# Keeping the split weight panels of the first token block in DRAM and loading them in the other three

## The chip, the cores and the metric

The kernel runs on one core of a Trainium2 chip. TensorE (PE) multiplies, VectorE (DVE), ScalarE (ACT) and GpSimd (POOL) do the elementwise work, and SyncE (SP) issues the DMAs, which all run on the core's 16 DMA engines. The metric is the time of one execution on the device in microseconds, the median of several; lower is better. Numbers are float32 throughout.

## The reference

One decoder layer works on 2048 tokens of width 1024. Cut to what matters here:

```
xn = RMSNorm(h);  z = xn @ W_in
o  = concat(GLA(z_gla), RWKV7(z_rwkv)) @ W_out ;  h += o
h += relu(RMSNorm(h) @ W1)^2 @ W2
h += sigmoid(RMSNorm(h) @ W_g) * (p @ W_p)
out = RMSNorm(h)
```

W1 is 1024 x 4096 and W2 4096 x 1024. GLA and RWKV7 are recurrent mixers that go through the tokens in order.

## The kernel before, in words

The tokens are cut into four blocks (0 to 3) of 512. All weights are cut into panels of 128 x 1024 numbers (512 KB): per block 26 of W_in (stage z), 8 of W_out (o), 64 of W1 and W2 (f) and 10 of W_g and W_p (p), that is 108 panels, and each is used once in each of the four blocks.

A matmul is done with float32r operands, a rounded form of float32 that goes faster. To keep the precision, each operand is split into a rounded part `hi` and the rest `lo`, and each product is three matmuls (L267 to L269): hi x hi, hi x lo, lo x hi. A panel is 8 such products of 128 x 128 against 512 tokens, so 24 matmuls. `load_w` (L237) fetches a panel to `wr` (3 buffers) and splits it in two halves: a cast on ACT to `wh` (L244) and a subtraction to `wl` (L247), on DVE, or in stage z in turn on DVE and POOL. `wh` and `wl` have 5 half-panel buffers each. This happens anew in every block, 432 times in all.

The order of the work: first stage z of block 0; then z of blocks 1 to 3, with the mixers of block 0 woven in between (`tick`, twice per panel); then the o, f and p stages of block 0, with the mixers of block 1 woven in; and so on; those of block 3 have no mixer beside them. Names in the trace begin with stage and block: z2, f0; r12 is the RWKV mixer of block 1, part 2 of 0 to 3, and g12 the GLA mixer of the same part. A part of the RWKV mixer computes an inverse row by row on DVE (L868, L871), writes it to DRAM in eight DMAs (`place`, L887 and L888), reads it back in another layout in ten (tiles `TT` and `rT`), and PE goes on with it (`join`, L913).

The program is written in this order, and a scheduler then fixes the order of the instructions of each engine before the run: each engine executes its list in order and waits at the first instruction whose operands, buffers or (for DMAs, in eight lanes in turn) an earlier DMA of its lane are not ready. All DMAs are on SP's list: weights, tokens, the mixers' operands, results. So an SP instruction that waits holds all transfers behind it.

Of the kernel before, what the change touches and what calls it, by code (L numbers as in the profile page):

```python
# [61 lines left out]
def tile_hybrid_block(ctx: ExitStack, tc: tile.TileContext, a: dict, out: bass.AP):  # L62
# [35 lines left out]

# [1 line left out]
    vec = ct([P, NV], "vec")  # L100
# [71 lines left out]

    # low-rank factors, split into exact float32r parts
    w2s = cx(TB, F32R)[:96]
# [22 lines left out]

# [1 line left out]
    gst = ct([P, 4, P], "gst")  # L199
# [15 lines left out]

# [1 line left out]
    def rsqrt(v, n, tag):  # L217
# [13 lines left out]

    loaded = []

    def take_w():
        return loaded.pop(0)

    def load_w(src):  # L237
        raw = st([P, 1024], "wr", 3)
        ld(raw, src)
        parts = []  # L240
        for x in range(2):
            r = raw[:, 512 * x : 512 * x + 512]
            hi, lo = st([P, 512], "wh", 5, F32R), st([P, 512], "wl", 5, F32R)
            A.copy(hi, r)  # L244
            eng = G if wcount[0] % 2 and stage[0][0] == "z" else V
            wcount[0] += 1
            eng.tensor_tensor(out=lo, in0=r, in1=hi, op=ALU.subtract)  # L247
            parts.append((hi, lo))
        return parts

    def xt():
# [66 lines left out]

# [1 line left out]
    lastc = {}  # L320
# [3 lines left out]
    def z_units(b):  # L324
# [264 lines left out]

        wz = a["w_z"]  # L590
        units += [(low_a, wz[NZ]), (low_b, wz[NZ + 1])]
# [5 lines left out]

# [1 line left out]
    def gla_units(b, j):  # L599
# [161 lines left out]

# [1 line left out]
    NJ = S // P  # L763
    dlt = [tc.dram_tile([32, 32, 32], F32, name=f"dlt{x}") for x in range(NJ)]
    dtt = [tc.dram_tile([32, 32, 32], F32, name=f"dtt{x}") for x in range(NJ)]
    dtp = [tc.dram_tile([16, 32, 32], F32, name=f"dtp{x}") for x in range(NJ)]
    # T^T per head; chunk parity q sits on rows 64 * (1 - q)
    TT = ct([P, 8, 64], "TT")
# [260 lines left out]

# [1 line left out]
    H = {}  # L1031

    def out_units(b):
# [26 lines left out]
        for n in range(KT):  # L1060
            u.append((f_(n), a["w_o"][n]))
        return named(f"o{b}", u)

    def ffn_units(b):
# [30 lines left out]
        def down(g, n):  # L1095
            def f():
                acc = panel(take_w(), s_[g])
                h = H[b]["h"][n]
                V.tensor_tensor(out=h, in0=h, in1=acc, op=ALU.add)
                if g == FF // P // FG - 1:  # L1100
                    H[b]["n"].add(h)
                    H[b]["xs"].append(split_x(h, vc("ln_ple", n)))
            return f

        for g in range(FF // P // FG):
            for i in range(FG):
                u.append((up(g, i), a["w_1"][g * FG + i]))
            for n in range(KT):
                u.append((down(g, n), a["w_2"][g, n]))
        return named(f"f{b}", u)  # L1110

    def ple_units(b):
# [41 lines left out]

        wg, wp = a["w_g"], a["w_p"]
        u.append((first, wg[0], wg[1], wp[0]))
# [156 lines left out]
```

## Time and profile before

| what | value |
|---|---|
| median of 3 timed runs | 2979.53 us (2975.93 to 2981.45) |
| profiled execution, first to last instruction (span) | 2978.2 us |
| TensorE busy | 2869.2 us, 96% |
| VectorE busy | 2295.4 us, 77% |
| ScalarE busy | 1265.4 us, 42% |
| DMA moved | 385.49 MB, 129 GB/s on the mean |

The profile gives the profiled execution's time as its span; nothing is recorded around it, and the timed median is 1.3 us longer. The stages follow each other like this: z0 until about 200 us, z1 to z3 with the mixers of block 0 until about 853, then the o, f and p stages of block 0 until 1395, of block 1 until 1944, of block 2 until 2494 and of block 3 until 2963. In the page, PEclk is the clock that TensorE was granted; 1.00 is 2.4 GHz, and a stretch at the lower level of 1.2 GHz draws the mean down. The DMA share is how busy the 16 DMA engines were.

### The profile page before, as it was taken

How to read it: one execution, taken by the hardware profiler on the slowest of the kernel's cores; microseconds unless marked ns; L12 is line 12 of the kernel's file. 1: busy time of each engine (PE TensorE's matmuls, PEld its weight loads, DVE VectorE, ACT ScalarE, POOL GpSimd, SP SyncE). 2: the span in 40 equal slices, each digit the busy share in tenths (PEclk: the TensorE clock that was granted, in tenths of full speed). 3: DMA queues.
4: the chain of work that ended last, by engine and by line, in shares of the span. 5: the costliest groups of instructions: out<-in, count | busy, mean ns of one | idle time of the engine just before them, and what ended most of it. 6: DMA issues, size and time to landing. Idle time of an engine off the chain costs nothing.

```text
span 2978.2 us, 47104 instructions
## 1 busy us (share of the span) xinstructions
PE 2869.2 (96%) x16856; PEld 2266.4 (76%) x16856; DVE 2295.4 (77%) x5495; ACT 1265.4 (42%) x2382; POOL 214.7 (7%) x347
## 2 busy tenths in 40 slices
PE   8998998899899999999999999999999999999998
PEld 6676776676777778787778778777878787888886
DVE  7899898888988768688968768787867787544455
ACT  6455555556543333344433334443333344322233
POOL 2332221222200000000000000000000000000000
PEclk9999999999999999999999999999999999999999
DMA  4464645544463333444533343454333334322222
GB/s 156 164 189 145 190 133 153 179 141 155 139 200 112 112 118 103 121 121 138 154 119 104 116 117 109 124 179 118 104 116 115 108 109 156 106 92 95 96 92 78
DMA packets 313835, 385.49 MB, mean 129 GB/s; under 512 B 132016, under 2 KB 213984, under 8 KB 313600
## 3 DMA queue, kind: packets, MB, share of 16 engines
q1 hardware_dynamic: 313600, 382.48, 41.2%
q8 instruction: 133, 2.18, 0.3%
q14 instruction: 102, 0.84, 0.1%
HBM read 316.32 MB, written 66.06 MB: 128 GB/s over the span
## 4 chain that ended last, share of the span: by engine, by line
PE 75%; DVE 10%; DMA 2%; issue 2%; ACT 1%; SPq 0%; POOL 0%; DVEq 0%; ACTq 0%; POOLq 0%
PE f0.mm L267 4%; PE f1.mm L267 4%; PE f3.mm L268 4%; PE f3.mm L269 4%; PE f3.mm L267 4%; PE f1.mm L269 4%; PE f0.mm L268 4%; PE f0.mm L269 4%; PE f1.mm L268 4%; PE f2.mm L267 4%; PE f2.mm L269 4%; PE f2.mm L268 4%; PE p1.mm L267 1%; PE p0.mm L267 1%; DVE z3.g L574 1%
## 5 line engine op out<-in xcount | busy, mean ns | idle before, releaser
L244 ACT CAST f3.wh<-f3.wr 128x512 fp32r<-128x512 f32 x128 | 79.5, 621 | 198.7 <-PE f3.mm L268 190.4
L244 ACT CAST f0.wh<-f0.wr 128x512 fp32r<-128x512 f32 x128 | 79.0, 618 | 153.6 <-PE f0.mm L268 121.0
L244 ACT CAST f1.wh<-f1.wr 128x512 fp32r<-128x512 f32 x128 | 79.0, 618 | 147.0 <-PE f1.mm L268 117.2
L244 ACT CAST f2.wh<-f2.wr 128x512 fp32r<-128x512 f32 x128 | 79.0, 618 | 146.1 <-PE f2.mm L268 115.6
L247 DVE TENSOR_TENSOR f3.wl<-f3.wr,f3.wh 128x512 fp32r<-128x512 f32 x128 | 88.0, 688 | 52.9 <-ACT f3.wh L244 52.9
L247 DVE TENSOR_TENSOR f0.wl<-f0.wr,f0.wh 128x512 fp32r<-128x512 f32 x128 | 87.8, 686 | 28.0 <-ACT f0.wh L244 27.9
L247 DVE TENSOR_TENSOR f1.wl<-f1.wr,f1.wh 128x512 fp32r<-128x512 f32 x128 | 87.7, 685 | 27.0 <-ACT f1.wh L244 26.9
L247 DVE TENSOR_TENSOR f2.wl<-f2.wr,f2.wh 128x512 fp32r<-128x512 f32 x128 | 87.7, 685 | 26.5 <-ACT f2.wh L244 26.4
L267 PE MATMUL f2.mm<-f2.x,f2.wh 128*128 128x512 f32 x256 | 103.6, 405 | 0.0
L267 PE MATMUL f1.mm<-f1.x,f1.wh 128*128 128x512 f32 x256 | 103.6, 405 | 0.0
L267 PE MATMUL f0.mm<-f0.x,f0.wh 128*128 128x512 f32 x256 | 103.5, 404 | 0.0
L268 PE MATMUL f1.mm<-f1.x,f1.wh 128*128 128x512 f32 x256 | 101.2, 395 | 0.0
L269 PE MATMUL f1.mm<-f1.x,f1.wl 128*128 128x512 f32 x256 | 101.1, 395 | 0.0
L269 PE MATMUL f0.mm<-f0.x,f0.wl 128*128 128x512 f32 x256 | 101.1, 395 | 0.0
L268 PE MATMUL f0.mm<-f0.x,f0.wh 128*128 128x512 f32 x256 | 101.0, 395 | 0.0
L268 PE MATMUL f2.mm<-f2.x,f2.wh 128*128 128x512 f32 x256 | 100.8, 394 | 0.0
L269 PE MATMUL f2.mm<-f2.x,f2.wl 128*128 128x512 f32 x256 | 100.8, 394 | 0.0
L269 PE MATMUL f3.mm<-f3.x,f3.wl 128*128 128x512 f32 x256 | 100.8, 394 | 0.0
L267 PE MATMUL f3.mm<-f3.x,f3.wh 128*128 128x512 f32 x256 | 100.7, 393 | 0.0
L268 PE MATMUL f3.mm<-f3.x,f3.wh 128*128 128x512 f32 x256 | 100.7, 393 | 0.0
L267 PE MATMUL f0.mm<-o0.x,f0.wh 128*128 128x512 f32 x248 | 100.6, 406 | 0.0
L267 PE MATMUL f1.mm<-o1.x,f1.wh 128*128 128x512 f32 x248 | 100.2, 404 | 0.0
(2804 smaller groups left out, 9164.8 us busy)
## 6 DMA issues: line engine op xcount, KB each, us to landing
f0.wr<-w SPq DMA_DIRECT2D x63, 512.0 KB, 3.3
f1.wr<-w SPq DMA_DIRECT2D x63, 512.0 KB, 3.4
f2.wr<-w SPq DMA_DIRECT2D x63, 512.0 KB, 3.3
f3.wr<-w SPq DMA_DIRECT2D x63, 512.0 KB, 3.3
z0.wr<-w_z SPq DMA_DIRECT2D x27, 512.0 KB, 3.8
z1.wr<-w_z SPq DMA_DIRECT2D x26, 512.0 KB, 3.6
z2.wr<-w_z SPq DMA_DIRECT2D x26, 512.0 KB, 3.9
z3.wr<-w_z SPq DMA_DIRECT2D x25, 512.0 KB, 3.6
```

The source lines that it names most:

```text
L244: A.copy(hi, r)
L247: eng.tensor_tensor(out=lo, in0=r, in1=hi, op=ALU.subtract)
L267: T.matmul(acc, wh, xs[0], start=start, stop=False)
L268: T.matmul(acc, wh, xs[1], start=False, stop=False)
L269: T.matmul(acc, wl, xs[0], start=False, stop=stop)
L574: V.scalar_tensor_tensor(o, x[:, j : j + TB], convh[:, 4 * i + j : 4 * i + j + 1], o, ALU.mult, ALU.add)
```

## The change

In block 0 each panel is loaded and split as before; the two split halves of a panel, now tiles of 128 x 1024 that hold `hi` beside `lo`, are then written to DRAM scratch, 512 KB each. The stores stand in SP's list behind the load of the next panel. In blocks 1 to 3 `load_w` loads these two tiles in place of the raw panel, and nothing is split. The tags `wr`, `wh` and `wl` become one tag `w` with 8 tiles of 4 KB per partition, the same 32 KB per partition as before; block 0 uses three of them per panel, the other blocks two.

```diff
+    wcache = {}
+    pending = []
...
+    def w_tile(dtype):
+        return st([P, 1024], "w", 8, dtype)
+
+    def store_w():
+        while pending:
+            dst, t = pending.pop(0)
+            nc.sync.dma_start(dst, t.bitcast(F32))
+
     def load_w(src):
-        raw = st([P, 1024], "wr", 3)
+        key, src = src
+        parts = []
+        if key in wcache:
+            store_w()
+            for x in range(2):
+                t = w_tile(F32R)
+                ld(t.bitcast(F32), wcache[key][x])
+                parts.append((t[:, :512], t[:, 512:]))
+            return parts
+        raw = w_tile(F32)
         ld(raw, src)
-        parts = []
+        store_w()
+        wcache[key] = []
         for x in range(2):
             r = raw[:, 512 * x : 512 * x + 512]
-            hi, lo = st([P, 512], "wh", 5, F32R), st([P, 512], "wl", 5, F32R)
+            t = w_tile(F32R)
+            hi, lo = t[:, :512], t[:, 512:]
             A.copy(hi, r)
             eng = G if wcount[0] % 2 and stage[0][0] == "z" else V
             wcount[0] += 1
             eng.tensor_tensor(out=lo, in0=r, in1=hi, op=ALU.subtract)
             parts.append((hi, lo))
+            d = tc.dram_tile([P, 1024], F32, name=f"wc_{key[0]}_{'_'.join(map(str, key[1:]))}_{x}")
+            wcache[key].append(d)
+            pending.append((d, t))
         return parts
```

The callers pass a key with each panel (`wsrc`); nothing else changes. The scheduler orders all engines anew. Line numbers after L230 move by 27 (L247 becomes L268, L913 becomes L940).

Three places show it. DVE's list in stage z2, around the convolutions of z2 (L574, later L601; g02 is the GLA mixer beside them), before:

```order
L574 SCALAR_TENSOR_TENSOR z2.g2_1324_5970<-z2.x_1322_5965,convh_96,z2.g2_1324_5970 128x512 [waits DMAHW5_49,Activation_49]
L663 TENSOR_TENSOR g02.gqk_1406_6336<-g02.gk_1277_5779,g02.ge_1405_6332 128x256 [waits PE_49]
L574 SCALAR_TENSOR_TENSOR z2.g2_1324_5970<-z2.x_1322_5965,convh_96,z2.g2_1324_5970 128x512 [waits DVE_49]
L658 TENSOR_TENSOR g02.ge_1407_6342<-g02.gb_1278_5780 128x64x2
L574 SCALAR_TENSOR_TENSOR z2.g2_1324_5970<-z2.x_1322_5965,convh_96,z2.g2_1324_5970 128x512 [waits DVE_49]
L247 TENSOR_TENSOR z2.wl_1372_6192<-z2.wr_1370_6189,z2.wh_1371_6191 128x512 [waits PE_49,Activation_49]
L659 TENSOR_TENSOR g02.ge_1407_6342<-g02.gb_1278_5780 128x64x2
L577 SCALAR_TENSOR_TENSOR z2.g2_1325_5975<-z2.g2_1325_5975,z2.g2_1324_5970 128x512 [waits Activation_49]
L295 TENSOR_TENSOR z3.nacc_1290_5812<-z3.nacc_1290_5812,z3.g2_1334_6028 128x512 [waits Activation_49]
L574 SCALAR_TENSOR_TENSOR z2.g2_1345_6078<-z2.x_1343_6073,convh_96,z2.g2_1345_6078 128x512 [waits DMAHW0_49,Activation_49]
L574 SCALAR_TENSOR_TENSOR z2.g2_1345_6078<-z2.x_1343_6073,convh_96,z2.g2_1345_6078 128x512 [waits DVE_49]
L247 TENSOR_TENSOR z2.wl_1392_6273<-z2.wr_1390_6270,z2.wh_1391_6272 128x512 [waits PE_49,Activation_49]
```

and now:

```order
L601 SCALAR_TENSOR_TENSOR z2.g2_1146_5770<-z2.x_1144_5765,convh_96,z2.g2_1146_5770 128x512 [waits DMAHW2_49,Activation_49,Pool_49]
L690 TENSOR_TENSOR g02.gqk_1216_6112<-g02.gk_1105_5591,g02.ge_1215_6108 128x256 [waits PE_49]
L601 SCALAR_TENSOR_TENSOR z2.g2_1146_5770<-z2.x_1144_5765,convh_96,z2.g2_1146_5770 128x512 [waits DVE_49]
L685 TENSOR_TENSOR g02.ge_1217_6118<-g02.gb_1106_5592 128x64x2
L601 SCALAR_TENSOR_TENSOR z2.g2_1146_5770<-z2.x_1144_5765,convh_96,z2.g2_1146_5770 128x512 [waits DVE_49]
L686 TENSOR_TENSOR g02.ge_1217_6118<-g02.gb_1106_5592 128x64x2
L604 SCALAR_TENSOR_TENSOR z2.g2_1147_5775<-z2.g2_1147_5775,z2.g2_1146_5770 128x512 [waits Activation_49]
L322 TENSOR_TENSOR z3.nacc_1118_5624<-z3.nacc_1118_5624,z3.g2_1156_5828 128x512 [waits Activation_49]
L601 SCALAR_TENSOR_TENSOR z2.g2_1164_5872<-z2.x_1162_5867,convh_96,z2.g2_1164_5872 128x512 [waits DMAHW7_49,Activation_49,Pool_49]
```

The two subtractions of weight halves (L247) are gone from between the steps of a convolution; the rest stands in the same order.

SP's list in the f stage of block 0, where part 2 of block 1's RWKV mixer (r12) writes its inverse to DRAM (dtt6, dtp6) and reads it back (TT); f0.wr is a raw weight panel, before:

```order
L97 DMA f0.wr_2828_13036<-w_2 128x1024 [waits DMAHW5_49,DMAHW2_49,DVE_49]
L887 DMA dtt6_191<-r12.rtt_2706_12445 256x1x32 [waits DVE_49,Pool_49]
L888 DMA dtp6_207<-r12.rpr_2792_12809 512x1x8 [waits DVE_49]
L887 DMA dtt6_191<-r12.rtt_2706_12445 256x1x32 [waits Pool_49]
L888 DMA dtp6_207<-r12.rpr_2792_12809 512x1x8 [waits DMAHW6_49]
L887 DMA dtt6_191<-r12.rtt_2706_12445 256x1x32 [waits DMAHW7_49,Pool_49]
L888 DMA dtp6_207<-r12.rpr_2792_12809 512x1x8 [waits DMAHW0_49]
L887 DMA dtt6_191<-r12.rtt_2706_12445 256x1x32 [waits DMAHW1_49,Pool_49]
L888 DMA dtp6_207<-r12.rpr_2792_12809 512x1x8 [waits DMAHW2_49]
L97 DMA f0.wr_2835_13083<-w_2 128x1024 [waits DMAHW3_49,DVE_49]
L97 DMA TT_217<-dtt6_191 32x4x32 [waits DMAHW5_49,DMAHW7_49,DMAHW4_49,DMAHW1_49]
```

and now, with f0.w the raw panel or a split tile and wc_ the scratch tile that it is stored to:

```order
L97 DMA f0.w_2412_12528<-w_2 128x1024 [waits DMAHW5_49,PE_49]
L245 DMA wc_w_2_2_2_0_12462<-f0.w_2401_12459 128x1024 [waits DMAHW3_49,DVE_49]
L914 DMA dtt6_191<-r12.rtt_2328_12119 256x1x32 [waits DMAHW4_49,DVE_49,Pool_49]
L915 DMA dtp6_207<-r12.rpr_2404_12493 512x1x8 [waits DVE_49]
L914 DMA dtt6_191<-r12.rtt_2328_12119 256x1x32 [waits DMAHW6_49,Pool_49]
L915 DMA dtp6_207<-r12.rpr_2404_12493 512x1x8 [waits DMAHW7_49]
L914 DMA dtt6_191<-r12.rtt_2328_12119 256x1x32 [waits DMAHW0_49,Pool_49]
L915 DMA dtp6_207<-r12.rpr_2404_12493 512x1x8 [waits DMAHW1_49]
L914 DMA dtt6_191<-r12.rtt_2328_12119 256x1x32 [waits DMAHW2_49,Pool_49]
L915 DMA dtp6_207<-r12.rpr_2404_12493 512x1x8 [waits DMAHW3_49]
L245 DMA wc_w_2_2_2_1_12466<-f0.w_2402_12463 128x1024 [waits DMAHW4_49,Activation_49]
L97 DMA TT_217<-dtt6_191 32x4x32 [waits DMAHW5_49,DMAHW6_49,DMAHW2_49,DMAHW0_49]
```

The mixer's eight stores and its reads keep their order. Between them stood the load of a raw panel; now the store of a split half stands there, and another such store stands right ahead of the eight.

PE's list at the same part, where the product that needs the read-back tiles (L913, later L940) stands among the matmuls of the panel f0.mm, before:

```order
L267 MATMUL f0.mm_2821_12968<-f0.x_2713_12482,f0.wh_2809_12886 128x512 [waits Activation_49]
L268 MATMUL f0.mm_2821_12968<-f0.x_2714_12483,f0.wh_2809_12886 128x512
L269 MATMUL f0.mm_2821_12968<-f0.x_2713_12482,f0.wl_2810_12887 128x512 [waits DVE_49]
L267 MATMUL f0.mm_2821_12968<-f0.x_2726_12536,f0.wh_2809_12886 128x512
L913 MATMUL r12.gx_2813_12904<-r12.rT11_2793_12819,r12.rgb_2631_12092 32x32 [waits DMAHW4_49,PE_49]
L913 MATMUL r12.gx_2813_12904<-r12.rT11_2793_12819,r12.rgb_2631_12092 32x32 x7
```

and now (the panel named here is the one before):

```order
L295 MATMUL f0.mm_2419_12578<-f0.x_2362_12289,f0.w_2414_12536 128x512
L296 MATMUL f0.mm_2419_12578<-f0.x_2361_12288,f0.w_2414_12536 128x512
L294 MATMUL f0.mm_2419_12578<-f0.x_2379_12365,f0.w_2414_12536 128x512
L295 MATMUL f0.mm_2419_12578<-f0.x_2380_12366,f0.w_2414_12536 128x512
L296 MATMUL f0.mm_2419_12578<-f0.x_2379_12365,f0.w_2414_12536 128x512
L940 MATMUL r12.gx_2421_12592<-r12.rT11_2405_12503,r12.rgb_2263_11756 32x32 [waits DMAHW5_49,PE_49]
L940 MATMUL r12.gx_2421_12592<-r12.rT11_2405_12503,r12.rgb_2263_11756 32x32 x7
```

The product stood in the 44th panel of stage f0, after 16 of its 24 matmuls; now it stands behind the last matmul of the 43rd.

## Rows read from the trace of the kernel before

**Rows 1.** The page: span and busy times, and the busy tenths of PE, DVE and the DMA engines in 40 equal slices of the span.

```profile
span 2978.2 us, 47104 instructions
PE 2869.2 (96%) x16856; PEld 2266.4 (76%) x16856; DVE 2295.4 (77%) x5495; ACT 1265.4 (42%) x2382; POOL 214.7 (7%) x347
...
PE   8998998899899999999999999999999999999998
DVE  7899898888988768688968768787867787544455
DMA  4464645544463333444533343454333334322222
```

**Rows 2.** Busy time of each engine by stage: z0; z1 to z3; the o, f and p stages of blocks 0, 1, 2 and 3. Columns: stretch, its length, then busy us (instructions) of PE, PEld, DVE, ACT and POOL, granted clock, DMA share, GB/s.

```profile
core 0: us, PE busy (x) PEld busy (x) DVE busy (x) ACT busy (x) POOL busy (x), PEclk, DMA share, GB/s
0.00:200.00 200.00, 177.25 (x791) 135.79 (x791) 162.09 (x312) 107.95 (x192) 59.83 (x104) 0.95 0.52 169
200.00:853.00 653.00, 594.73 (x3690) 456.02 (x3690) 578.58 (x1438) 359.80 (x696) 144.72 (x176) 0.96 0.50 158
853.00:1395.00 542.00, 541.40 (x3417) 430.48 (x3418) 425.82 (x1093) 212.71 (x413) 3.61 (x24) 1.00 0.40 119
1395.00:1944.00 549.00, 546.12 (x3464) 434.79 (x3464) 435.81 (x1121) 215.49 (x418) 3.62 (x24) 1.00 0.41 123
1944.00:2494.00 550.00, 544.40 (x3450) 433.73 (x3448) 433.01 (x1103) 212.75 (x411) 2.88 (x19) 1.00 0.40 120
2494.00:2963.00 469.00, 463.61 (x2028) 374.31 (x2028) 251.90 (x413) 155.52 (x252) 0.00 (x0) 0.99 0.31 102
```

**Rows 3.** The waits of PE in the stretch 200 to 853 us: the three costliest, and the one on a split weight. Columns: engine and instruction, whom it waited for, us in total, times, longest.

```profile
PE z1.gx L549 <- DVE z1.g L535: 7.5, 4, 2.8
PE z2.gx L451 <- ACT z2.x L446: 6.9, 1, 6.9
PE z2.gx L549 <- DVE z2.g L535: 6.3, 4, 3.2
PE z2.mm L269 <- DVE z2.wl L247: 1.9, 1, 1.9
```

**Rows 4.** The chain of waits that ended last, by line, as shares of three stretches: 200 to 400, 400 to 600 and 600 to 853 us.

```profile
by line: DVE z1.g L574 6.4%; PE z1.mm L267 5.6%; PE z1.mm L268 5.5%; PE z1.mm L269 5.5%; issue 4.5%; DVE z1.wl L247 2.6%; PE z1.gx L549 2.2%; DVE z1.g L535 2.0%; DVE z1.g L524 1.9%; DVE z1.g L533 1.6%; PE r01.gx L809 1.6%; DVE z1.g L532 1.4
by line: issue 8.0%; PE z2.mm L268 5.5%; PE z2.mm L269 5.0%; PE z2.mm L267 4.6%; DVE r01.rpr L868 3.8%; DMA z3.g<-xT 3.7%; DVE z2.wl L247 2.6%; DVE r01.rtt L871 2.4%; DMA g02.gk<-d_gk 2.3%; DVE qz L667 2.2%; DMA d_ar<-z2.g 2.1%; PE z2.gx L5
by line: DVE z3.g L574 7.5%; issue 7.1%; PE z3.mm L267 5.9%; PE z3.mm L269 5.8%; PE z3.mm L268 5.8%; PE z2.mm L269 2.5%; DVE r03.rpr L868 2.4%; DVE z3.wl L247 2.3%; PE z2.mm L268 2.2%; PE z2.mm L267 2.1%; DMA o0.g<-d_o 1.8%; DVE z2.g L574 1
```

**Rows 5.** The split alone, for z0, z1 to z3 and block 0: stretch, length, busy us (instructions) of the subtractions (L247) on DVE and on POOL, granted clock, DMA share, GB/s; behind the dots the casts (L244; busy us of ACT) from 200 to 853 us.

```profile
0.00:200.00 200.00, 20.95 (x29) 41.34 (x28) 0.95 0.52 169
200.00:853.00 653.00, 55.43 (x79) 116.07 (x77) 0.96 0.50 158
853.00:1395.00 542.00, 111.81 (x163) 0.00 (x0) 1.00 0.40 119
...
200.00:853.00 653.00, 94.85 (x156) 0.96 0.50 158
```

**Rows 6.** Three stretches (columns as in rows 2): late in z0; block 3's f stage, where the DMAs are weight loads and little else; the end, where they are result stores and nothing else. Then issues of DMAs: count, KB each, median us from issue to landing.

```profile
140.00:180.00 40.00, 36.87 (x167) 29.61 (x166) 35.87 (x57) 18.88 (x34) 16.99 (x21) 0.96 0.78 232
2600.00:2800.00 200.00, 200.00 (x865) 162.04 (x865) 91.66 (x141) 54.67 (x88) 0.00 (x0) 1.00 0.28 95
2966.00:2978.00 12.00, 1.08 (x4) 0.71 (x4) 6.78 (x17) 0.59 (x1) 0.00 (x0) 0.53 0.46 175
...
outT<-o3.h SPq DMA_DIRECT2D x8, 256.0 KB, 2.1
f0.wr<-w SPq DMA_DIRECT2D x63, 512.0 KB, 3.3
TT<-dtt SPq DMA_DIRECT2D x128, 16.0 KB, 2.6
```

**Rows 7.** SP's instructions around the mixer part r12 in block 0's f stage (start, us), and PE's product that needs what they fetch (durations in ns, first and last start in us).

```profile
1183.65 0.61 SPq L887 DMA_DIRECT2D dtt<-r12.rtt  x1
...
1188.31 0.61 SPq L888 DMA_DIRECT2D dtp<-r12.rpr  x1
1189.02 0.56 SPq L97 DMA_DIRECT2D f0.wr<-w  x1
1189.75 4.58 SPq L97 DMA_DIRECT2D TT<-dtt  x8
1194.38 1.08 SPq L97 DMA_DIRECT2D r12.rT<-dtp  x2
...
L913 PE MATMUL r12.gx<-r12.rT,r12.rgb x32: 191/191/212, 1196.8 to 1198.3; 32*32 32x32 f32 x32
```

**Rows 8.** Waits of PE from 853 to 2963 us: the two longest, and those on the read-back of a mixer part.

```profile
PE p2.gx L273 <- DVE p2.nacc L295: 3.5, 1, 3.5
PE o2.mm L267 <- ACT o2.x L257: 2.5, 1, 2.5
PE r31.gx L913 <- DMA r31.rT<-dtp: 0.4, 1, 0.4
PE r33.gx L913 <- DMA r33.rT<-dtp: 0.4, 1, 0.4
```

More of the change, by code (lines that the diff above doesn't have):

```diff
@@ L248, in load_w, with wsrc @@
             parts.append((hi, lo))
-        return parts
+            d = tc.dram_tile([P, 1024], F32, name=f"wc_{key[0]}_{'_'.join(map(str, key[1:]))}_{x}")
+            wcache[key].append(d)
+            pending.append((d, t))
+        return parts
+    def wsrc(name, *at):
+        return (name, *at), a[name][at if len(at) > 1 else at[0]]
     def xt():
@@ L588, in gate @@
             return f
-        wz = a["w_z"]
+        wz = [wsrc("w_z", i) for i in range(NZ + 2)]
         units += [(low_a, wz[NZ]), (low_b, wz[NZ + 1])]
@@ L1060, in out_units @@
         for n in range(KT):
-            u.append((f_(n), a["w_o"][n]))
+            u.append((f_(n), wsrc("w_o", n)))
         return named(f"o{b}", u)
@@ L1106, in ffn_units @@
             for i in range(FG):
-                u.append((up(g, i), a["w_1"][g * FG + i]))
+                u.append((up(g, i), wsrc("w_1", g * FG + i)))
             for n in range(KT):
-                u.append((down(g, n), a["w_2"][g, n]))
+                u.append((down(g, n), wsrc("w_2", g, n)))
         return named(f"f{b}", u)
@@ L1153, in f_ @@
             return f
-        wg, wp = a["w_g"], a["w_p"]
+        wg, wp = [wsrc("w_g", n) for n in range(KT)], [wsrc("w_p", n) for n in range(2)]
         u.append((first, wg[0], wg[1], wp[0]))
```

## The prediction

> **What bounds the kernel now.** I read the page first, then the stages, then for each stage what PE waited for and the chain of waits. The page has PE busy for 96% of 2978.2 us, DVE for 77%; in the slices DVE is at 8 or 9 in the first third and falls off behind it [rows 1]. By stage there are two regimes [rows 2]. In blocks 0 to 3's o, f and p stages PE is busy for 541.4 of 542, 546.1 of 549, 544.4 of 550 and 463.6 of 469 us, at a granted clock of 0.99 to 1.00: nothing but PE's own work counts there, and that work the change leaves alone. From 200 to 853 us, in z1 to z3 with block 0's mixers, PE is busy for 594.7 of 653 us and DVE for 578.6, 89% each, and the clock is 0.96: PE idles 58.3 us and loses another 4%, 26 us, to stretches at the lower level. So 84 us are there at most. PE's waits there are nearly all on DVE and ACT, on products of the z stage (7.5, 6.9 and 6.3 us are the largest), and hardly on split weights themselves: 1.9 us [rows 3]. But the chain passes through DVE's list, and the weight subtraction is on it with 2.6% of 200, 2.6% of 200 and 2.3% of 253 us [rows 4], that is 5.2 + 5.2 + 5.8 = 16 us. It stands in the way of other work rather than being waited for.
>
> **What goes in z1 to z3.** 79 subtractions on DVE (55.4 us), 77 on POOL (116.1 us) and 156 casts on ACT (94.9 us) [rows 5]. The smallest gain is what lies on the chain, 16 us. The largest that DVE's share allows: were it as busy as before (578.6/653 = 0.886) with 55.4 us less to do, the stage would take 523.2/0.886 = 590 us, 63 less; PE's 84 is a cap above that. I take 34: twice the chain's own pieces, because the 156 casts and the POOL subtractions, slower than DVE's (116.1/77 = 1.5 us against 0.7), delay the same chain and the three shares cut off above count only DVE.
>
> What comes in: loading parts moves two transfers of 512 KB per panel where one was. A load costs 1.55 us of all engines: at 95 GB/s, 200 us hold 36 loads, in 0.28 x 200 = 56 us [rows 6]. 78 panels add 121 us, and the DMA share goes from 0.50 to 0.69. The chain already has transfers on it: 3.7%, 2.3% and 2.1% of 200 us and 1.8% of 253 [rows 4], 21 us. If these stretch with the share by 0.69/0.50, that is 8 us; if they hide, nothing; I take 4. Stage z1 to z3: -34 + 4 = -30, from -63 to -8.
>
> **What comes in z0.** The split stays, and 26 panels are stored twice. A store is cheaper than a load: 8 result tiles of 256 KB took 0.46 x 12 = 5.5 us, so 1.38 us for 512 KB [rows 6]. 52 of them are 72 us, and the share rises from 0.52 [rows 2] to 0.88. On the mean that fits; from 140 to 180 us, at 0.78 already [rows 6], it asks for 1.14, and 0.14 x 40 = 6 us are over. That is my value. It is 0 if the panels loaded ahead cover it, and 24 if a third of the 26 raw loads are late by the two stores in front of them (26 x 2.76 / 3).
>
> **What comes in block 0.** PE has no idle time there, so each late operand costs its full delay. 82 panels stored twice are 226 us of DMA in 542, 0.40 + 0.42 = 0.82. The panels themselves are safe: the load of one waits for PE to be through half of the panel three before it, two and a half panels of 24 x 0.23 us ahead (0.23 = 200/865 [rows 6]), which is 14 us against a landing of 3.3 us [rows 6] and 2.76 us of stores ahead. The mixer parts are not. For r12, SP issues the first store at 1183.65 and the last read at 1194.38 + 1.08 us, and PE begins at 1196.8, as soon as the data can be there [rows 7]; no such wait was longer than 0.4 us [rows 8], so the order fits the trip exactly, without slack. The trip has two hops, and in the new order of SP a half-panel store stands ahead of each: 2 x 1.38 = 2.8 us, for four parts 11 us. That is my value. If two stores lie ahead of each hop (5.5 us) and the product, which now stands 16 matmuls (3.7 us) earlier in PE's list, is waited for from there, it is 4 x 9.2 = 37; if DVE reaches the inverse earlier, 0.
>
> The Trainium skill, DMA: Bandwidth & Descriptors, section "Latency and other measured facts", puts HBM access at 0.2 us on the mean and 2 us at high load, and speaks against the change at this place. The trace has TT's reads landing in 2.6 us at a share near 0.40 [rows 6], and no run here shows them at 0.82. By the page, an estimate: 1.8 us more on each of two hops in four parts, 14 us on top, and a sum of -2 instead of -16.
>
> **Blocks 1 to 3 and the end.** Here the splits cost PE little: it idles 2.9 + 5.6 + 5.4 us [rows 2], and the longest waits are on a norm on DVE and on the split of the attention output on ACT at the change of block, 3.5 and 2.5 us [rows 8], with weight splits in the same lists. Without these I take 3 us off. DMA goes to about 0.40 + 127/549 = 0.64, and the mixers' trips get a load more in front; DVE, some 112 us lighter per block [rows 5], covers that by being earlier. From -8 to +8. The 15 us behind 2963 keep their work.
>
> **Sum.** -30 + 6 + 11 - 3 = -16 us on the profiled 2978.2, so 2962. The timed median lay 1.3 us above that span; I predict 2963.
>
> **Rivals.**
> - The first block pays it all back (slower). The place is the read-back of the four mixer parts in block 0. With 37 us there, 6 in z0, 3 off in blocks 1 to 3 and 20 off in z1 to z3, the sum is +20, 2999. For it: no slack in rows 7, and a DMA share of 0.82. Against: at 0.50 with bursts of 0.78 the transfers of z still kept up. It decides once a part waits more than (30 + 3 - 6)/4 = 7 us.
> - Hidden anyway. Only the 16 us on the chain go, and z0 and block 0 take 6 + 11: +1, about 2980. For it: PE's waits on split weights are 1.9 us [rows 3]. [...]
> - The z stages fall to DVE's pace: -63 there, and -63 + 6 + 5 - 3 = -55, 2925. For it: DVE, ACT and POOL all get lighter, and fewer idle spells of PE also give back clock. Against: PE would then be left 21 us of idle and slow time of 84.
>
> **Chances.** My forecast 0.42, the slower rival 0.27, hidden anyway 0.18, DVE's pace 0.13. A measurement of this kernel tells about 0.2%, 6 us, from no change. Faster by more: 0.42 + 0.13 = 0.55; within: 0.18; slower: 0.27. The likeliest case alone runs from 2940 to 2972. The range for 8 in 10 takes in DVE's pace and most of the slower rival: 2922 to 3003.
>
> **What would show it.** From 200 to 853 us: no L247 or L244 successor on any engine in z1 to z3, DVE busy near 523 us, the stage ending about 25 us sooner, its clock above 0.96. In z0 a DMA share near 0.9 and the stage's end 6 us later. In block 0, waits of PE on the read-back of r10 to r13 of about 3 us each; over 7 us makes me wrong, and so do waits of PE on a weight load, which I count at nothing. In blocks 1 to 3, lengths within 8 us in all.

## The result: slower by 1.4%, and the profile after

The median of four timed runs is 3021.1 us (3014.7 to 3028.8), against 2980.0 for the kernel before in the same session: a ratio of 1.014, 95% interval 1.012 to 1.016. The prediction of 2963 us, faster, was wrong, and the time lies above its range.

The page of the changed kernel, the lines that answer to [rows 1]:

```profile
span 3013.0 us, 45970 instructions
PE 2878.3 (96%) x16856; PEld 2271.0 (75%) x16856; DVE 1922.1 (64%) x4925; ACT 887.1 (29%) x1738; POOL 91.0 (3%) x269
...
PE   7888999999999999999999999999999999999998
DVE  7767786969785757677856557676645665322234
...
DMA  7787776877777676777766666676566556555553
```

DVE lost 373 us of work and ACT 378 us, and the kernel got slower. The DMA row is at 5 to 8 nearly throughout, where it was at 2 to 6. PE's row shows the loss in its first four slices only; behind these a 9 is 90% or more, and what block 0 lost hides in that. By stage, the columns of [rows 2]:

```profile
0.00:224.80 224.80, 181.97 (x798) 133.11 (x799) 165.34 (x308) 108.13 (x191) 56.21 (x103) 0.95 0.79 272
224.80:825.90 601.10, 576.32 (x3700) 448.34 (x3699) 474.25 (x1364) 284.60 (x546) 24.77 (x99) 0.98 0.76 241
825.90:1434.90 609.00, 573.35 (x3417) 451.55 (x3416) 433.06 (x1081) 204.02 (x412) 3.60 (x24) 0.96 0.74 249
1434.90:1984.80 549.90, 540.58 (x3482) 431.15 (x3481) 348.58 (x972) 117.66 (x252) 3.60 (x24) 1.00 0.65 205
```

Between first products of stages (the first matmul of z1, of o0, o1, o2 and o3; z0 from the start, block 3 to the end of the span) the profiled executions last, in us:

| kernel | z0 | z1 to z3 | block 0 | block 1 | block 2 | block 3 | span |
|---|---|---|---|---|---|---|---|
| before | 200.0 | 653.3 | 546.7 | 550.4 | 548.7 | 479.1 | 2978.2 |
| after | 224.8 | 601.1 | 609.0 | 549.9 | 550.7 | 477.5 | 3013.0 |
| difference | +24.8 | -52.2 | +62.3 | -0.5 | +2.0 | -1.6 | +34.8 |

The spans differ by 34.8 us and the timed medians by 41: the profiled execution of the changed kernel was the fastest of its four.

So the gain came, larger than forecast, and block 0 took it all and more. Block 0 before, between the same two products (the stretch in [rows 2] ends 5 us ahead of the second):

```profile
853.30:1400.00 546.70, 543.75 (x3454) 432.41 (x3453) 430.48 (x1102) 214.68 (x417) 3.61 (x24) 1.00 0.40 121
```

Of block 0's 609 us PE is idle for 36, where it was idle for 3 before: 33 us more. And it is busy for 30 us longer with the same work, at a clock of 0.96 where it was 1.00; 0.04 x 609, 24 us, is an estimate of what the clock took of these. What PE waited for in block 0 (826 to 1435 us; for [rows 8]):

```profile
PE f0.mm L294 <- ACT f0.w L265: 7.9, 4, 3.4
PE o1.mm L294 <- ACT o1.x L284: 4.0, 1, 4.0
PE g13.gx L668 <- DVE qz L694: 2.8, 1, 2.8
PE g11.gx L654 <- DMA g11.gv<-d_gv: 2.6, 1, 2.6
PE o0.mm L294 <- ACT o0.w L265: 2.3, 1, 2.3
PE g12.gx L300 <- DVE g12.gqk L641: 2.2, 1, 2.2
PE g13.gx L654 <- DMA g13.gv<-d_gv: 2.2, 1, 2.2
PE g12.gx L654 <- DMA g12.gv<-d_gv: 2.1, 1, 2.1
PE f0.mm L296 <- DVE f0.w L268: 1.7, 1, 1.7
...
PE r10.gx L940 <- DMA r10.rT<-dtp: 1.2, 2, 0.9
...
PE r12.gx L940 <- DMA r12.rT<-dtp: 1.1, 2, 1.0
```

The read-back of a mixer part, the place of the forecast's 11 us, is in the last two of these rows: 2.3 us. Waits on a split weight (f0.w, o0.w) are 11.9 us, a third of the 36; the GLA mixers' operands from DRAM (gv) are 6.9, and the rest is mostly work of VectorE and ScalarE, for the mixers above all. How much of that rest is late for the same reason as the weights, these rows do not tell. The longest wait is on a weight panel whose cast (L265) was late, and ACT's own waits say why the cast was late:

```profile
ACT f0.w L265 <- DMA f0.w<-w: 33.7, 20, 4.4
```

The raw panel had not landed. SP's waits in the same stretch show where it was:

```profile
SPq L245 <- DVE f0.w L268: 187.8, 66, 10.4
SPq L245 <- DVE p0.w L268: 29.2, 15, 5.5
SPq L245 <- DVE o0.w L268: 22.9, 7, 11.0
```

For 240 of 609 us SP's list stands at a store (L245) that waits until DVE has split its panel. Whatever is behind the store in the list waits too, the next raw panel and the mixers' operands among it. A piece of the list (start in us, duration):

```profile
1117.42 0.56 SPq L97 DMA_DIRECT2D g12.gv<-d_gv  x1
1118.08 0.56 SPq L97 DMA_DIRECT2D f0.w<-w  x1
1118.69 0.90 SPq L245 DMA_DIRECT2D wc_w<-f0.w  x2
1119.68 1.00 SPq L97 DMA_DIRECT2D f0.w<-w  x1
1129.27 0.92 SPq L245 DMA_DIRECT2D wc_w<-f0.w  x2
...
1135.12 0.38 SPq L97 DMA_DIRECT2D f0.w<-w  x1
```

From 1120.7 to 1129.3 nothing is issued, and the next raw panel goes out at 1135.1. And the loads land later than before (issues, KB, median us to landing; [rows 6] had 3.3 for a raw panel in f0):

```profile
wc_w<-f0.w SPq DMA_DIRECT2D x126, 512.0 KB, 4.0
f0.w<-w SPq DMA_DIRECT2D x63, 512.0 KB, 5.7
```

The theories after this: (A) the ring of eight tiles, in which a raw panel needs a tile whose store must have landed; (B) the bytes, 152 MB in block 0; (C) for z1 to z3, GpSimd's subtractions had been slowing VectorE; (D) late raw loads, held by SP's list or by the ring. The rival from the start was the order of SP's list alone.

### The profile page after: what moved, and what is told of

It reads as the page before. It is cut to its first block, busy times and chain, and to the rows that moved or that the text cites. A ratio compares the mean times of both kernels' runs of the same rounds, so it can differ in the third digit from the quotient of the medians.

```text
span 3013.0 us, 45970 instructions
## 1 busy us (share of the span) xinstructions
PE 2878.3 (96%) x16856; PEld 2271.0 (75%) x16856; DVE 1922.1 (64%) x4925; ACT 887.1 (29%) x1738; POOL 91.0 (3%) x269
## 4 chain that ended last, share of the span: by engine, by line
PE 67%; DVE 17%; DMA 7%; ACT 4%; issue 3%; SPq 2%; POOL 0%; DVEq 0%; ACTq 0%; POOLq 0%
PE f3.mm L295 4%; PE f3.mm L296 4%; PE f3.mm L294 4%; PE f2.mm L294 4%; PE f1.mm L294 4%; PE f2.mm L296 3%; PE f2.mm L295 3%; PE f1.mm L296 3%; PE f1.mm L295 3%; PE f0.mm L294 2%; PE f0.mm L296 2%; PE f0.mm L295 2%; SPq L97 1%; DVE f0.w L268 1%; PE z2.mm L294 1%
## 5 line engine op out<-in xcount | busy, mean ns | idle before, releaser
L294 PE MATMUL z0.mm<-z0.h,z0.w 128*128 128x512 f32 (+1 forms) x208 | 87.3, 420 | 28.9 <-ACT z0.w L265 21.3
L294 PE MATMUL f0.mm<-f0.x,f0.w 128*128 128x512 f32 x256 | 105.8, 413 | 5.7 <-ACT f0.w L265 5.7
L1126 DVE TENSOR_TENSOR o3.h<-o3.h,f3.mm 128x512 f32<-128x512 f32 x32 | 22.0, 688 | 132.8 <-PE f3.mm L296 132.8
L294 PE MATMUL f1.mm<-f1.x,f1.w 128*128 128x512 f32 x256 | 104.6, 408 | 1.0 <-ACT f1.x L284 1.0
L294 PE MATMUL f2.mm<-f2.x,f2.w 128*128 128x512 f32 x256 | 104.5, 408 | 0.4 <-ACT f2.x L284 0.4
L294 PE MATMUL f0.mm<-o0.x,f0.w 128*128 128x512 f32 x248 | 101.7, 410 | 2.2 <-ACT f0.w L265 2.2
L296 PE MATMUL f0.mm<-f0.x,f0.w 128*128 128x512 f32 x256 | 102.5, 400 | 0.0
L295 PE MATMUL f0.mm<-f0.x,f0.w 128*128 128x512 f32 x256 | 102.2, 399 | 0.0
L296 PE MATMUL f0.mm<-o0.x,f0.w 128*128 128x512 f32 x248 | 100.0, 403 | 1.8 <-DVE f0.w L268 1.7
L296 PE MATMUL f3.mm<-f3.x,f3.w 128*128 128x512 f32 x256 | 101.1, 395 | 0.0
L295 PE MATMUL f2.mm<-f2.x,f2.w 128*128 128x512 f32 x256 | 100.6, 393 | 0.5 <-DVE f2.x L285 0.5
L296 PE MATMUL f1.mm<-f1.x,f1.w 128*128 128x512 f32 x256 | 101.0, 395 | 0.0
L295 PE MATMUL f1.mm<-f1.x,f1.w 128*128 128x512 f32 x256 | 100.6, 393 | 0.4 <-DVE f1.x L285 0.4
L296 PE MATMUL f2.mm<-f2.x,f2.w 128*128 128x512 f32 x256 | 100.9, 394 | 0.0
L294 PE MATMUL f2.mm<-o2.x,f2.w 128*128 128x512 f32 x248 | 100.9, 407 | 0.0
L294 PE MATMUL f3.mm<-f3.x,f3.w 128*128 128x512 f32 x256 | 100.8, 394 | 0.0
L295 PE MATMUL f3.mm<-f3.x,f3.w 128*128 128x512 f32 x256 | 100.7, 394 | 0.0
L294 PE MATMUL f1.mm<-o1.x,f1.w 128*128 128x512 f32 x248 | 100.4, 405 | 0.0
L295 PE MATMUL f0.mm<-o0.x,f0.w 128*128 128x512 f32 x248 | 99.8, 402 | 0.0
L295 PE MATMUL f3.mm<-o3.x,f3.w 128*128 128x512 f32 x248 | 98.3, 396 | 0.0
L296 PE MATMUL f1.mm<-o1.x,f1.w 128*128 128x512 f32 x248 | 98.3, 396 | 0.0
```

Source lines behind the costliest of these rows:

```text
L294: T.matmul(acc, wh, xs[0], start=start, stop=False)
L295: T.matmul(acc, wh, xs[1], start=False, stop=False)
L296: T.matmul(acc, wl, xs[0], start=False, stop=stop)
```

## The experiments

Stage lengths, in the manner of the table above, for all of them; "time" is the median, of one run where no interval stands:

| run | z0 | z1 to z3 | block 0 | time | ratio to before |
|---|---|---|---|---|---|
| e1_no_store | 208.1 | 595.2 | 556.8 | 2941.6 | |
| e2_small_store | 215.2 | 597.4 | 557.0 | 2952.9 | |
| e6_half_bytes | 203.1 | 606.0 | 558.9 | 2953.5 | |
| e11_four_fifths | 215.4 | 600.9 | 563.3 | 2960.0 | |
| e3_pool_queue | 231.3 | 599.5 | 606.1 | 3020.1 | 1.012 (1.009 to 1.015) |
| e5_own_raw | 227.8 | 600.4 | 606.4 | 3016.6 | |
| e13_early | 230.1 | 598.3 | 595.8 | 3009.2 | |
| e14_own_and_queue | 210.3 | 606.6 | 582.7 | 2979.3 | |
| e10_relieved | 206.0 | 602.1 | 583.5 | 2973.0 | |
| e4_z_only | 230.6 | 599.3 | 553.7 | 2972.2 | 0.996 (0.995 to 0.997) |
| e8_z_own_raw | 226.8 | 604.9 | 549.8 | 2956.9 | 0.991 (0.988 to 0.993) |
| e9_z_in_turn | 203.9 | 617.6 | 548.9 | 2952.4 | 0.990 (0.987 to 0.992) |
| e7_dve_only | 184.9 | 641.1 | 548.3 | 2951.4 | |
| e12_z_low_only | 205.2 | 615.2 | 546.2 | 2939.7 | 0.985 (0.982 to 0.987) |
| e15_low_dve | 190.0 | 605.8 | 545.9 | 2920.4 | 0.980 (0.978 to 0.982) |
| e16_turn_dve | 191.9 | 631.8 | 548.1 | 2946.1 | 0.988 (0.986 to 0.990) |

Block 3 lies between 476.3 and 479.4 us in all of them, and blocks 1 and 2 between 548.0 and 554.1. A stage length is that of the one profiled execution, so differences of a few us between two runs may be chance.

**How many stores, and how many bytes (e1, e2, e6, e11).** e1 stores only the first four panels; to have the same loads, the later blocks fetch the parts of those four in place of the others'. e2 issues all 216 stores, but 208 of them (not the 212 of its expectation) with 64 KB; e6 and e11 store the first part of each panel in full and 64 or 320 KB of the second.

```diff
# e1
-                ld(t.bitcast(F32), wcache[key][x])
+                ld(t.bitcast(F32), wcache[full[pick[key]]][x])
...
+        pick[key] = len(pick) % 4
...
+        keep = len(full) < 4
+        if keep:
+            full.append(key)
...
+            if not keep:
+                continue
# e2, with pick, full and the loads of e1
+            cols = slice(0, 1024) if keep else slice(448, 576)
-            nc.sync.dma_start(dst, t.bitcast(F32))
+            nc.sync.dma_start(dst[:, cols], t[:, cols].bitcast(F32))
# e6, against e2
-                ld(t.bitcast(F32), wcache[full[pick[key]]][x])
+                ld(t.bitcast(F32), wcache[key if x == 0 else full[pick[key]]][x])
...
-            pending.append((d, t, keep))
+            pending.append((d, t, keep or x == 0))
# e11, against e6
-            cols = slice(0, 1024) if keep else slice(448, 576)
+            cols = slice(0, 1024) if keep else slice(192, 832)
```

> Only the first 4 panels are stored, and blocks 1 to 3 load the parts of these four in place of their own, so the sums are over other weights; the number and size of loads stay, the 8-tile ring stays, 208 of 216 stores go. If the stores cost the time (by their bytes or by their place in SP's list), z0 goes from 225 to about 200 us and block 0 (825.9 to 1434.9) from 609 to about 547 us, about 2930 us in all. If the ring costs it (three of eight tiles per panel in block 0, fewer panels ahead than with the old buffers), block 0 stays near 609 us and the total near 3000.

> All 216 stores are issued, each behind its wait for the split, but 212 of them carry 128 of 1024 columns (64 KB in place of 512 KB); loads as in the run without stores, from the first four panels. If bytes on the DMA engines cost the time, this is as fast as without stores (about 2930 us, block 0 about 547 us). If the waits of SP in front of the stores cost it, whatever the bytes, block 0 stays near 609 us and the total near 3015. In between, both.

> Of each panel the first split part is stored in full (512 KB), of the second only 64 KB (except for four panels, whose second parts blocks 1 to 3 load in place of the others', so the output is wrong there); as many stores as in the changed kernel, 56% of the bytes. Theory B with a cost in proportion to bytes: block 0 lies halfway, between 557 (64 KB stores) and 609 us, at 580 to 588, z0 at about 220, the sum 2978 to 2990. Theory B with a threshold (only what the engines cannot carry is paid for): block 0 at 557 to 565, z0 at 216 to 219, the sum 2950 to 2962. Theory A (the ring): the store of the first part holds its tile as before and the second is let go early, so about halfway too, 575 to 590.

> As the run with 56% of the bytes, but of the second split part 320 KB are stored instead of 64: 81% of the changed kernel's bytes in as many stores (output wrong as there). Theory B with a threshold: block 0 gets dearer from some point between 559 us (56%) and 609 us (100%); if that point is near the middle, block 0 takes 570 to 590 us and the sum is 2965 to 2985. If the cost were a matter of order or buffers and not of bytes, it would stay at 557 to 562.

Without stores block 0 takes 557 us, with all of them at 64 KB 557.0 too: that a store is there, and that SP waits for the split before it, costs nothing measurable. Nor do the waits further up tell by themselves what PE pays. In e1 ScalarE waits longer for raw panels than in the changed kernel (33.7 us), and in e2 SP still stands at f0's stores, each with block 0 at 557:

```profile
ACT f0.w L271 <- DMA f0.w<-w: 81.4, 38, 9.2
```

```profile
SPq L248 <- DVE f0.w L275: 89.3, 33, 5.3
```

At 56% of the bytes it is 559, at 81% 563, at 100% 609. The stretch in e6 and then in e11 (columns as in [rows 2]):

```profile
809.10:1368.00 558.90, 548.72 (x3444) 437.50 (x3443) 428.39 (x1099) 206.23 (x410) 3.58 (x24) 0.99 0.66 207
```

```profile
816.30:1379.60 563.30, 547.90 (x3443) 437.23 (x3442) 429.90 (x1099) 206.11 (x411) 3.62 (x24) 0.99 0.75 245
```

So the bytes of the stores make the difference, and nearly all of their cost comes between 81 and 100%; my guess of proportion (580 to 588 for e6) and of a point near the middle (570 to 590 for e11) both missed. The share does not show it: e11 moves 245 GB/s at a share of 0.75, the changed kernel 249 at 0.74 in 46 us more. The 10 us between 557 and before's 547 have nothing to do with stores. z0 does not follow the bytes: from none to all it takes 208, 215, 203, 215 and 225 us; why, is open.

**What holds the loads: ring, list or engines (e3, e5, e13, e14, e10).** e3 issues the stores from GpSimd's list. e5 gives the raw panels their three buffers back and the parts five. e13 is e5 with each raw panel fetched one panel earlier; e14 is e5 and e3 together; e10 all three.

```diff
# e3, e10, e14
-            nc.sync.dma_start(dst, t.bitcast(F32))
+            nc.gpsimd.dma_start(dst, t.bitcast(F32))
# e5, e10, e13, e14
-        raw = w_tile(F32)
+        raw = st([P, 1024], "wr", 3)
...
-        return st([P, 1024], "w", 8, dtype)
+        return st([P, 1024], "w", 5, dtype)
# e10, e13: in run(), behind the loads of the panels that are split now
+                if got < len(srcs) and srcs[got][0] not in wcache and srcs[got][0] not in fetched:
+                    fetched[srcs[got][0]] = fetch_w(srcs[got])
```

> The same 216 stores of 512 KB, issued on GpSimd's queue instead of SP's: bytes as in the changed kernel, SP's list free of the stores and of their waits. If SP's list is the cause (the mixers' loads held behind the stores), block 0 falls from 609 to about 550 us and the total to about 2955. If the bytes are, block 0 stays near 609 us and the total near 3015. GpSimd also does half of the subtractions in z0, so z0 may keep its 25 us, or lose more.

> The changed kernel with all its stores and loads, but raw panels get three buffers of their own and the split parts five (32 KB per partition as before); in blocks 1 to 3 loaded parts go through both kinds in turn, so eight tiles as now. Theory A, the ring of buffers: block 0 and z0 are long because a raw panel waits for a tile whose store has to land first. Then block 0 falls from 609 to 560 to 575 us, z0 from 225 to about 212, the sum to 2950 to 2965. Theory B, the bytes: the DMA engines cannot bring the raw panels in time beside 512 KB stores, whichever buffers they go to. Then block 0 stays at 600 to 610, z0 at 222 or more, and the sum is 3005 to 3020.

> The changed kernel with all that can keep a raw panel waiting taken away, and all bytes kept: raw panels have three buffers of their own, the stores are issued from GpSimd's list, and a raw panel is fetched one panel earlier. Theory B, capacity: the engines carry about 300 GB/s at best, and block 0 asks for 152 MB; then block 0 stays at 590 to 610 us and the sum above 2995. Theory D, lateness: the engines have room (mean share 0.74), and a load that starts earlier is there in time; then block 0 falls to 550 to 570, z0 to 205 to 215, the sum to 2940 to 2965.

> The changed kernel with own raw buffers and raw panels fetched one panel earlier, but the stores on SyncE's list again. Theory D, lateness of the raw loads: the earlier fetch alone is what helped, block 0 takes 580 to 590 us as with the stores on GpSimd, and PE waits at the read-backs instead of on panels. Rival: a store that waits for its split holds the earlier fetch on SyncE's list, and block 0 is back at 600 to 609 us.

> The changed kernel with own raw buffers and the stores on GpSimd's list, raw panels fetched when they were. If the earlier fetch is what helped: block 0 at 598 to 608 us. If it was that neither buffers nor SyncE's list hold a raw load any more: 580 to 590.

Each of the first two alone leaves block 0 at 606 us, and by each alone its theory would have fallen. Together they bring 582.7 and z0 from 225 to 210. In e3 SP no longer stands at stores, but ACT waits longer for raw panels than in the changed kernel (block 0, for the row of ACT above):

```profile
ACT f0.w L265 <- DMA f0.w<-w: 147.0, 49, 9.5
```

In e5 the list still holds the raw loads (SP waits 180.0 us for f0's splits, 187.8 in the changed kernel); in e3 what still holds them is the ring, since with buffers of their own added, in e14, they come in time (ScalarE waits 10.4 us for those of f0). So it needs both out of the way. e14 came out as its second case; e13, at 596, fell between its two, and e10, at 583.5, between capacity and lateness. Fetching a panel earlier brings 11 us on SP's list (e13 against e5) and nothing on top of e14 (e10). With the panels in time, PE waits in block 0 of e14 like this:

```profile
PE r12.gx L946 <- DMA r12.rT<-dtp: 6.2, 1, 6.2
PE r13.gx L946 <- DMA r13.rT<-dtp: 5.6, 1, 5.6
PE r11.gx L946 <- DMA r11.rT<-dtp: 5.6, 1, 5.6
PE o0.mm L300 <- ACT o0.x L290: 4.6, 1, 4.6
PE r10.gx L946 <- DMA r10.rT<-dtp: 3.1, 1, 3.1
```

This is the wait of the forecast, 20.5 us in four parts. It does not lie hidden behind a larger one in the changed kernel: there the way from SP's first store of r12's inverse to PE's product is 12.1 us, where it was 13.1 before [rows 7], and in e14 it is 18.4. First the changed kernel, then e14:

```profile
1189.40 0.60 SPq L914 DMA_DIRECT2D dtt<-r12.rtt  x1
1201.49 0.44 PE L940 MATMUL r12.gx<-r12.rT,r12.rgb 32*32 32x32 f32 x16 [0.97 <-DMA r12.rT<-dtp]
```

```profile
1161.97 0.60 SPq L920 DMA_DIRECT2D dtt<-r12.rtt  x1
1169.88 0.55 SPq L921 DMA_DIRECT2D dtp<-r12.rpr  x1
1180.37 0.64 PE L946 MATMUL r12.gx<-r12.rT,r12.rgb 32*32 32x32 f32 x16 [6.22 <-DMA r12.rT<-dtp]
```

In e14 the eight small stores alone take 8.5 us to issue, 5.3 before; why, is open. e14's block 0 as a stretch:

```profile
816.90:1399.60 582.70, 557.77 (x3447) 445.01 (x3446) 429.93 (x1097) 211.76 (x412) 87.88 (x183) 0.97 0.80 259
```

Freeing list and ring took 26 us off block 0; it is still 33 us above the 549.8 of e8, which has the same buffers and no stores there. Issuing the stores does not slow VectorE: f0's subtractions take at most 695 ns in e14, 703 before. Whether these 33 us would be the same with the stores on a list other than GpSimd's, no run shows. That the DMA engines can carry no more than these 259 GB/s is not shown, and z0 speaks against it: in e10 it carried 303, with its own raw loads and full stores:

```profile
0.00:206.00 206.00, 171.56 (x791) 131.49 (x791) 161.16 (x310) 104.71 (x188) 82.87 (x155) 0.98 0.86 303
```

**What z1 to z3 gained from (e7).** The kernel before, with one edit:

```diff
-            eng = G if wcount[0] % 2 and stage[0][0] == "z" else V
+            eng = V
```

> The kernel before, with all weight subtractions of the z stages on VectorE and none on GpSimd; nothing is stored. Theory C: GpSimd's subtractions made VectorE's own instructions longer, and that is the half of VectorE's saving in z1 to z3 (104 us where 55 were counted) which the subtractions themselves do not explain. Then the 77 subtractions more (54 us) are paid for by about 49 us that the other instructions lose, VectorE is busy for 575 to 595 us from z1 to z3, a convolution step (L574) takes 749 ns instead of 884 to 974, and z1 to z3 last 645 to 660 us. Rival: the two do not touch each other, L574 stays near 900 ns, VectorE is at 630 us and the stage at 690 us or more.

VectorE does 78 subtractions more from z1 to z3 and is busy for less, 554.7 us instead of 578.6 [rows 2]:

```profile
184.90:826.00 641.10, 602.22 (x3699) 462.15 (x3698) 554.72 (x1521) 363.89 (x701) 32.48 (x98) 0.95 0.52 162
```

The convolution steps (L574; ns least/median/most, then first and last start) before, and then in e7:

```profile
L574 DVE SCALAR_TENSOR_TENSOR z1.g<-z1.x,convh,z1.g x24: 734/741/1807, 340.2 to 395.4; 128x512 f32<-128x512 f32 x24
L574 DVE SCALAR_TENSOR_TENSOR z2.g<-z2.x,convh,z2.g x24: 732/744/1799, 563.2 to 616.7; 128x512 f32<-128x512 f32 x24
```

```profile
L574 DVE SCALAR_TENSOR_TENSOR z1.g<-z1.x,convh,z1.g x24: 733/743/754, 323.6 to 377.4; 128x512 f32<-128x512 f32 x24
L574 DVE SCALAR_TENSOR_TENSOR z2.g<-z2.x,convh,z2.g x24: 734/742/751, 539.4 to 583.5; 128x512 f32<-128x512 f32 x24
```

The median is the same, and the slow ones are gone: up to 1.07 us more, somewhat less than a subtraction on GpSimd took (1.32 to 1.38 us as a median). Before, 14 of the 72 steps of z1 to z3 take 1.19 us or more, and in the trace every one of them overlaps such a subtraction, for 0.6 to 1.3 us. So theory C holds, and more than its size: I had expected VectorE at 575 or more. The kernel gains 12 us in z1 to z3 and 15 in z0, and this one line changed in the kernel before is worth 32 us (2951.4, one run, against 2983.5).

**Storing only the z panels (e4, e8, e9).** e4 stores no o, f and p panels. e8 does so with e5's buffers. In e9 z0 stores every second panel, and z1 splits and stores the rest.

```diff
# e4, e8
+        keep = key[0] == "w_z"
# e9
+        keep = key[0] == "w_z" and (stage[0] == "z1" or key[1] % 2 == 0)
```

> Only the panels of stage z are stored and loaded as parts; o, f and p panels are split in every block as before the change. If stages add up as the two traces differ (z0 +25, z1 to z3 -52, blocks 0 to 3 as before), the total is about 2953 us, 0.991 of before. If the gain in z1 to z3 needs lighter splits later on, or block 0's loss comes from z, it is 2980 or more.

> Only the z panels are stored and loaded again, and raw panels get their three buffers back beside five tiles of split parts, as the kernel before has them. Theory A: the 7, 4 and 4 us that blocks 0 to 2 lost in the z-only run with one ring of eight come back, and z0 falls from 231 to 210 to 215: 2978 - 53 + 12 = 2937. Theory B: the blocks come back, z0 stays at 228 or so: 2978 - 53 + 28 = 2953. Rival: with five tiles of parts the z panels come late in z1 to z3, which takes 610 or more: 2965.

> As the z-only kernel with raw buffers of its own, but z0 stores every second panel only and z1 splits and stores the others. Theory B: z0 has half the stores and loses 10 to 14 us in place of 28; z1 splits 13 panels and stores 13 MB, where DVE and DMA have room: z1 to z3 take 605 to 612 instead of 600; the sum is 2942 to 2950, below the kernel that stores all in z0. Theory A: z0 is at 208 to 212 in either case, and this one is 5 to 10 us slower than the other.

All three beat both kernels, e4 by least, 0.4% against the kernel before. e4 missed its 2953 by 19 us, since z0 lost 31 and not 25 and blocks 0 to 2 lost 14 in all. e4's blocks 0 to 2 are 7, 4 and 4 us longer than before, and with the three raw buffers in e8 these shrink, by 4, 6 and 2 us: that may be what the ring costs where nothing is stored, but it is little above chance between single executions, and whether block 0's 10 us in e1 are the same, no run shows. z0 does not gain from the buffers alone (227 against 231), as block 0 did not in e5. Half the stores bring z0 to 204 (e9), and z1 to z3, which take the other half, to 618 (605 to 612 expected, so that the time lies 2 us above the forecast); the sum of both, 821.5, is 10 us below e8's.

**Half the bytes, and no subtraction on GpSimd (e12, e15, e16).** e12 stores the lo halves alone; z1 to z3 load the raw panel and these, and cast hi. e15 and e16 are e12 and e9 with e7's edit.

```diff
             A.copy(hi, r)
+            parts.append((hi, lo))
+            if known:
+                ld(lo.bitcast(F32), known[x])
+                continue
```

> The kernel before with its buffers, but z0 stores the lo parts of its panels alone (256 KB a half panel), and z1 to z3 load the raw panel and the two lo parts and cast hi on ScalarE: half the stores in z0, as many bytes loaded in z1 to z3, no weight subtraction there. By the run with 56% of the bytes z0 and z1 to z3 together take 810 to 815 us against 853 before and 821 where z1 stores the other half; the blocks stay as before: 2938 to 2946, the fastest so far. Rival: the 156 casts on ScalarE were part of the chain; then z1 to z3 take 615 to 625 and the sum is 2950 to 2960.

> As the z-only kernel that stores the lo parts alone, with the weight subtractions of z0 on VectorE instead of half of them on GpSimd. By the run without GpSimd's subtractions z0 gains 15 us: 190 instead of 205; z1 to z3 have no such subtractions and stay at 615; the sum is 2945 - 15 = 2930, and 2924 to 2932 as a median. Rival: in z0 the stores now set the pace, z0 stays at 200 to 205 and the sum at 2940.

> As the kernel whose z0 stores every second z panel and z1 the others, with all weight subtractions on VectorE. z0 gains up to 15 us of 204, z1 gains up to 8 us because GpSimd no longer stretches VectorE's work there: 2950 - 23 = 2927; at least 2935 if z0 is bound by its stores. It lies within 10 us of the kernel that stores lo parts alone.

e12 came out within its forecast, but with z1 to z3 at its rival's 615. e15 is 2.0% faster than the kernel before, the best of all: z0 at 190.0, only 5 us above e7's, and the blocks as before. Its first two stretches:

```profile
0.00:190.00 190.00, 173.63 (x792) 132.06 (x792) 154.35 (x335) 107.90 (x192) 22.74 (x77) 0.97 0.76 256
190.00:795.80 605.80, 579.44 (x3699) 449.34 (x3699) 481.28 (x1366) 355.72 (x694) 20.55 (x98) 0.99 0.75 237
```

It fell 4 us below its forecast, with z1 to z3 at 606 instead of e12's 615 without any edit to them. Part of that is the choice of execution: e12's profiled one was the slowest of its four, 7.5 us above their median, and e15's the fastest; the rest is open. e16 missed the other way: z0 as expected, but z1 to z3 at 632 in its profile, where e9 had 618. Its order of instructions is another one, and I did not find out what in it costs these 14 us (its profiled execution lies 4.7 us above the median of its four).

## Why the prediction was wrong

**Block 0, +11 (0 to 37): measured +62.** This is the step that failed, and in it the sentence "the panels themselves are safe". It set 14 us of lead, from when a raw buffer comes free, against a landing of 3.3 us and the transfer of two stores, 2.76 us. But a load goes out when SP's list comes to it, and in front of it stood stores that waited for a split, for 187.8 us in f0; it needs a tile of a ring whose stores have to land first; and it landed after 5.7 us. PE's waits on split weights, counted at nothing and named as a sign of being wrong, were 11.9 us. The runs divide the 62 like this: from 547 to 550 with the old buffers and no stores in block 0 (e8), to 583 with full stores that hold neither SP's list nor the raw panels' buffers (e14), to 609 with the list and the ring shared. So 33 us came with the full stores as such, on GpSimd's list, and 26 with loads and stores sharing list and ring. Taking away only the list's hold or only the ring's left block 0 at 606, and with both in place 81% of the bytes cost no more than 563. I had the number, a share of 0.82 expected, and read it as below 1 and so as room; it became 0.74, because the same bytes took longer.

A second term was at nothing: "each late operand costs its full delay", and no more. Of the 62 us 33 are more idle time of PE and 30 longer matmuls, most of these by the clock, 0.96 for 1.00 (24 us by the estimate above).

**The read-backs** were the forecast's place, and there the sum of 11 us was wrong too: in the changed kernel they are 2.3 us in all, since the way of r12 did not get longer, although a half-panel store stood in it. In e14 they are 3.1 to 6.2 us, where I took 2.8 and bounded at 9.2, but behind small stores that issue more slowly, not behind a half-panel store on SP's list. So the slower rival was right in its sign and wrong in its place; a part never waited its 7 us, and the kernel got slower all the same. By the Trainium skill, DMA: Bandwidth & Descriptors, section "Latency and other measured facts", each hop would have grown by 1.8 us, an estimate from its 0.2 and 2 us. TT's reads in block 0 have a median landing of 3.1 us before, 2.1 in the changed kernel and 3.5 in e14, at shares of 0.40, 0.74 and 0.80. These runs do not bear it out.

**z1 to z3, -30 (-63 to -8): measured -52.** Right in sign; the term -34 was too small. VectorE was forecast at 523 us and came to 474: subtractions were 53 of the 104 us that it lost, and the other half was the stretch that GpSimd's subtractions had given to its other work. I had counted these 116 us of GpSimd as slow, not as a load on VectorE. The Trainium skill states it, SBUF — State Buffer, section "SBUF: two separate sides": the two engines share a pair of ports, and an instruction of GpSimd, or one of VectorE with two inputs in SBUF, as the convolution step has, takes it for its whole length while the other stands. The 1807 against 741 ns above agree with that; the rule was there to read, and I did not weigh it. e7 has 12 of the 52 us by this alone. How the other 40 divide between casts, subtractions and order, the runs do not tell: with the casts kept, z1 to z3 took 615 in e12 and 606 in e15.

**z0, +6 (0 to 24): measured +24.8**, just above the upper end, and for the reason given with it: late raw loads. PE waited on casts of z0's panels, ten times:

```profile
PE z0.mm L294 <- ACT z0.w L265: 21.3, 10, 7.3
```

In e14 none of PE's larger waits in z0 is of this kind, and z0 is at 210; the list and the ring held the loads here too.

**Blocks 1 to 3, -3: measured -0.1** (-0.5 + 2.0 - 1.6). Right: VectorE lost 87 us in block 1 and the block kept its length; the DMA share was 0.65, 0.64 forecast.

With these three terms at their measured sizes the sum comes out: 25 - 52 + 62 = +35 us of span.

## What to carry to other kernels

A transfer that waits in a queue holds everything behind it, so for each added store ask what it waits for and what stands behind it, before asking how long it takes; and if two things hold a load, taking away either alone shows nothing. A mean DMA share below 1 does not tell how much room there is where loads and stores wait for each other, and the cost can come as a cliff: 81% of the bytes here cost 6.5 us of block 0, the rest 46, at shares of 0.75 and 0.74. A wait further up, of ScalarE for a panel or of SP at a store, is not yet a cost: e1 and e2 have such waits and lose 10 us. Before saving VectorE's work, see whether its instructions run longer while GpSimd works beside it: moving GpSimd's subtractions to VectorE was worth 32 us here, without a byte stored.

## What was not expected of the hardware

- Between 81% and 100% of the stored bytes block 0 grew by 46 us, and from 0 to 81% by 6.5. The rate was 245 to 259 GB/s in e11, the changed kernel and e14, although e10's z0 carried 303 for 206 us.
- An idle microsecond of PE cost up to nearly a second one: in block 0 of the changed kernel it idled 33 us more and its matmuls took 30 us more, at a granted clock of 0.96, that is with part of the time at the lower level of 1.2 GHz; in e14 22 and 14 us, at 0.97.
- GpSimd busy for 7% of the span cost the kernel before about 1%: VectorE's 128x512 steps took up to 1.8 us beside its subtractions and at most 0.75 without them.
